# Four different start addresses for the low halves of four groups of weights

## The chip, the core and the metric

The kernel runs on one core of one Trainium2 chip. The metric is the device time of one execution in microseconds (us); the time of a kernel is the median of its runs. Matmuls run on TensorE (PE in the profile, with its weight loads shown apart as PEld), elementwise work on VectorE (DVE) and ScalarE (ACT), and transfers are issued by SyncE (SP).

## The reference, cut to what matters

One decoder layer in float32 for 256 rows of width 2048:

```python
h = rmsnorm(x, pre_mix_gain)
q_sb, k_sb, v_sb, q_dl, k_dl, v_dl = split(h @ w_in)
mixed = concat(head_rmsnorm(stick_breaking(...)), head_rmsnorm(dilated(rope...)))   # 8 + 8 heads of 128
x = x + rmsnorm(mixed @ w_out, post_mix_gain)
h = rmsnorm(x, pre_ffn_gain)
u = causal_depthwise_conv3(h @ w_up) + conv_b        # 2 x 5504 columns: gate and value
f = (gelu(gate) * value) @ w_down
x = x + rmsnorm(f, post_ffn_gain)
```

Only the products `h @ w_in` (its query and key columns) and `h @ w_up` (gate and value) meet the change.

## The kernel before, in words

**Precision by halves.** TensorE multiplies in float32r, a rounded form. To come close to float32, each operand is split into a high part, its value rounded to float32r, and a low part, the rest. A product is then three products: high by high, high by low, low by high. `high` (L86 to L89) makes the high half `wh` of a block of weights on ScalarE, `low` (L91 to L96) the low half `wl` on VectorE, as raw minus high.

**Chunks.** The weights come in chunks of 128 partitions by 2048 columns (two loads of 1024), in the order of the list `chunks` (L169 to L183): value columns of attention (`v`), then query and key for each head (`qk`, where the third entry `s` is 0 for query and 1 for key), then the output projection (`out`), then gate and value for each of 43 blocks of the feed-forward network (`up`, `s` 0 for gate, 1 for value). The main loop (L742) takes them one after another; `ahead` (L187) issues loads two chunks ahead and makes the high and low halves one chunk ahead.

**Which operand is which.** For `v`, `out` and the down projection the weights are the moving operand: they stream through the array in 512 columns, and a 128x128 block of activations is stationary, loaded ahead of each matmul. For `qk` and `up` it is the other way round, in `mm_stationary` (L98 to L107): a 128x128 block of weights is stationary and the transposed activations `hT` move. For each chunk it issues 16 matmuls with blocks of `wh` against 512 moving columns (high and low activations side by side, L103), then 16 with blocks of `wl` against 256 columns (the high activations alone, L107). 32 chunks of `qk` (16 query, 16 key) and 84 of `up` (42 gate, 42 value) go this way; the first gate and value chunk go through `mm_stationary_late` (L109), which mixes blocks of `wh` and `wl` in another order with 256 moving columns each (L113).

**Where the tiles lie.** `hT` holds 2048 bytes for each of 16 row blocks, so every moving operand starts at the same byte modulo 512. Blocks of weights are 512 bytes wide (128 columns of 4 bytes), so the blocks of a tile all start at the same byte modulo 512, too. In the compiled program `hT` starts at byte 384 of the partition, the four `wh` buffers at 57728, 61824, 65920 and 70016, the four `wl` buffers at 74112, 78720, 83328 and 87936: all of them 384 modulo 512. `low` can place its result further into the buffer, by `at` columns; each `wl` buffer has 128 columns (512 bytes) of room for this. Before the change `at` is 80 columns (320 bytes) for `qk` and `up` and 0 for all others. So high blocks lie 0 bytes behind the moving operand and low blocks 320 bytes, modulo 512.

Of the kernel before, what the change touches and what calls it, by code (L numbers as in the profile page):

```python
# [51 lines left out]
def layer_kernel(ctx: ExitStack, tc: tile.TileContext, a, out: bass.AP):  # L52
# [15 lines left out]
            tc.keep_in_program_order(ins)  # L68
        return ins

    HALF, LOW_AT = 1024, 80

    def load(src, w, piece=HALF):
        raws = []
# [7 lines left out]
    def split(raws, kind):  # L82

        return [low(raw, high(raw), kind) for raw in raws]
# [5 lines left out]

    def low(raw, wh, kind=None):  # L91

        at = LOW_AT if kind in ("qk", "up") else 0
        wl = wpool.tile([P, at + raw.shape[1]], F32R, tag="wl", name="wl", bufs=4, padded_shape=[P, HALF + P])[:, at:]
        pin(V.tensor_tensor(wl, raw, wh.bitcast(F32), op=ALU.subtract))  # L95
        return wh, wl  # L96
# [72 lines left out]
    chunks = []  # L169
# [14 lines left out]
    raws, parts_of, between = {}, {}, {}  # L184
    LOADS, SPLITS = 2, 1

    def ahead(i, splits=SPLITS):  # L187
        if i + LOADS >= len(chunks):
            down.load(2 * (i + 1 + LOADS - len(chunks)))
        if i + 1 == len(chunks):  # L190
            down.prepare(2)
        while len(raws) < min(len(chunks), i + 1 + LOADS):
            j = len(raws)
            if j in between:
                nc.sync.dma_start(*between[j])
            raws[j] = load(chunks[j][3], chunks[j][4])
        while len(parts_of) < min(len(chunks), i + 1 + splits):
            j = len(parts_of)
            parts_of[j] = split(raws[j], chunks[j][0])
        return parts_of[i]  # L200


# [82 lines left out]
    for i in range(1, 4):  # L285
        load_x(4 * i, 4 * i + 4)
        for j in range(2 * i, 2 * i + 2):
            raws[j] = load(chunks[j][3], chunks[j][4])
        split_x(4 * i, 4 * i + 4)
        if i == 1:  # L290
            parts_of[2] = split(raws[2], chunks[2][0])
    tc.keep_in_program_order(nc.sync.dma_start(ident, a["cst"][:, C_ID:C_END]))
    between[8] = (x1[:, 0, :], a["x"][0:P, :])
    between[9] = (x1[:, 1, :], a["x"][P:S, :])
# [447 lines left out]
    for i, (kind, p, s, _, w) in enumerate(chunks):  # L742
# [40 lines left out]
        elif kind == "out":  # L783
            if s == 0:
                mm["out", p] = [ps_mm.tile([P, 512], F32, tag="mm", name="mmo") for _ in range(2)]
                if rows is None:
                    nc.sync.dma_start(gbc, a["gpost"][0:1, :].partition_broadcast(P))
                    rows = Rows(mg, "o")
            if p == 3 and s == 2:
                held = parts  # L790
                continue
            if p < 3 or s < 2:
                mm_moving(mm["out", p], parts, mix[0], mix[1], 4 * s, s == 0, s == 3)
                if s == 3:
                    for t in range(2):
                        rows.squares(mm["out", p][t], t, p)
                        rows.take(mm["out", p][t], t, p)
            else:
                pinned[0] = True
                up0 = []  # L800
                r = [None, None]
                sq = Rows(None, "n")

                def square(t, *cs):
                    for c in cs:
                        sq.squares(x1[:, t, col(c)], t, c)

                def keep(t):
                    nc.sync.dma_start(x1_kept[t * P:(t + 1) * P, :], x1[:, t, :])

                pts = {}
                col = lambda c: slice(c * 512, (c + 1) * 512)

                def update(t, c, lo=0, hi=512):
                    cs = slice(c * 512 + lo, c * 512 + hi)
                    pin(V.scalar_tensor_tensor(x1[:, t, cs], mg[:, t, cs], r[t], x1[:, t, cs], op0=ALU.mult, op1=ALU.add))

                def turn(t, b):
                    if b not in pts:
                        pool, tag = (ps_mm, "mm") if b in (4, 5) else (ps_at, "at")  # L820
                        pts[b] = pool.tile([P, 2, S], F32, tag=tag, name="pth")
                    for j in range(2):
                        k = 2 * b + j
                        pin(T.transpose(pts[b][:, j, t * P:(t + 1) * P], x1[:, t, k * P:(k + 1) * P], ident))

                def highs(b):
                    for j in range(2):
                        k = 2 * b + j
                        gp = par[:, P_FFN + k:P_FFN + k + 1]
                        pin(A.activation(hT[0][:, k, :], pts[b][:, j, :], AF.Copy, scale=gp))  # L830

                def lows(b):
                    for j in range(2):
                        k = 2 * b + j
                        gp = par[:, P_FFN + k:P_FFN + k + 1]
                        pin(V.scalar_tensor_tensor(hT[1][:, k, :], pts[b][:, j, :], gp, hT[0][:, k, :].bitcast(F32),
                                                   op0=ALU.mult, op1=ALU.subtract))

                for t in range(2):
                    mm_moving(mm["out", p], held + parts, mix[0], mix[1], 8, False, True, (t,))  # L840
                    if t == 1:
                        for b in range(6):
                            turn(0, b)
                    rows.squares(mm["out", p][t], t, p)
                    vr = rows.mean(t)
                    rows.take(mm["out", p][t], t, p)
                    r[t] = rows.newton(*vr)
                    if t == 0:
                        for c in range(4):
                            update(0, c)  # L850
                        hs = [high(raw) for raw in raws[i + 1]]
                        up0.append(low(raws[i + 1][0], hs[0], "up"))
                        hs.append(high(raws[i + 2][0]))
                        square(0, 0)
                square(0, 1)
                update(1, 0, 0, 256)
                update(1, 0, 256, 512)
                update(1, 1)
                for b in range(2):
                    turn(1, b)  # L860
                    highs(b)
                update(1, 2)
                for b in range(2, 4):
                    turn(1, b)
                    highs(b)
                hs.append(high(raws[i + 2][1]))
                update(1, 3)
                up0.append(low(raws[i + 1][1], hs[1], "up"))
                parts_of[i + 1] = up0
                for b in range(4, 6):  # L870
                    turn(1, b)
                    highs(b)
                    lows(b - 4)
                    for t in range(2):
                        turn(t, b + 2)
                square(0, 2)
                highs(6)
                highs(7)
                square(0, 3)
                raws[i + 3] = load(chunks[i + 3][3], chunks[i + 3][4])  # L880
                hs.append(high(raws[i + 3][0]))
                square(1, 0, 1)
                hs.append(high(raws[i + 3][1]))
                square(1, 2, 3)
                lows(2)
                lows(3)
                parts_of[i + 2] = [low(raws[i + 2][0], hs[2], "up")]
                for b in range(4, 8):
                    lows(b)
                parts_of[i + 2].append(low(raws[i + 2][1], hs[3], "up"))  # L890
                parts_of[i + 3] = [low(raw, h, "up") for raw, h in zip(raws[i + 3], hs[4:])]
                keep(0)
                keep(1)
                pinned[0] = False
                phA.__exit__(None, None, None)
                phB = ctx.enter_context(tc.tile_pool(name="phB", bufs=2))
                yt = [phB.tile([P, len(SINGLES), S], F32R, name=f"yt{i}", bufs=1) for i in range(2)]
                yp = [phB.tile([P, NPAIR, 7, P], F32R, name=f"yp{i}", bufs=1) for i in range(2)]
        else:
            ps = ps_mm.tile([P, 2, S], F32, tag="mm", name="mmu")  # L900
            if p == 0 and s == 0:
                held = [(ps, parts)]
                continue
            if p == 0:
                held.append((ps, parts))
                mm_stationary_late(held, hT2)
                pinned[0] = True
                r2B = second_norm()
                pinned[0] = False
                convolved(held[0][0], 0, 0)  # L910
            else:
                mm_stationary(ps, parts, hT2)
            convolved(ps, p, s)
# [83 lines left out]
```

## Time and profile before

| what | value |
|---|---|
| median of 3 runs | 1103.24 us (1102.65 to 1103.39) |
| profiled execution, its own time | 1103.41 us |
| its span in the profile | 1101.5 us |
| mean granted clock of TensorE | 0.998 |
| PE, PEld, DVE, ACT busy | 99%, 85%, 79%, 61% of the span |
| L103 (high blocks, gate and value) | 1344 matmuls |
| L107 (low blocks, gate and value) | 1344 matmuls |
| L103 and L107, query and key | 512 matmuls each |

Matmuls overlap in the records: a matmul is shown from its start until its last result is out, and the next one starts before that. So the duration of one says little about the pace, and the busy time of a run of n matmuls is n-1 steps from start to start and one duration.

### The profile page before, as it was taken

The numbers are of one execution on the slowest core, as the hardware profiler recorded it, in microseconds if no ns is written. First come the engines' busy times: TensorE is split into PE (matmuls) and PEld (weight loads), VectorE is DVE, ScalarE is ACT, GpSimd is POOL, SyncE is SP. The second block draws the span as 40 slices with busy tenths as digits, with TensorE's granted clock in tenths as the row PEclk, the third lists the DMA queues.
The fourth block names the chain that finished last, engine by engine and source line by source line (L and its number), as shares of the span: only waits on it lengthen the run. The fifth ranks groups of instructions, "written<-read, shape, count | busy, mean of one in ns | idle before, by whom it ended". The sixth has DMA issues, their size and how long they took to land.

```text
span 1101.5 us, 16267 instructions
## 1 busy us (share of the span) xinstructions
PE 1089.8 (99%) x5855; PEld 940.5 (85%) x5855; DVE 872.3 (79%) x1371; ACT 668.0 (61%) x1046; POOL 5.3 (0%) x12
## 2 busy tenths in 40 slices
PE   9999999999999999999999999999999999999996
PEld 6888888888988888888888888888888888888885
DVE  6577776776876588978888878888878898889887
ACT  6656665655654476656666656665556566666665
POOL 0000000000000000000000000000000000000001
PEclk9999999999999999999999999999999999999999
DMA  8978787878889756655555555555556677778775
GB/s 308 385 251 303 254 264 264 289 264 269 290 281 305 260 191 210 191 192 191 192 191 191 191 192 191 189 190 192 184 195 186 192 251 249 249 225 250 246 244 210
DMA packets 75394, 257.80 MB, mean 234 GB/s; under 512 B 8496, under 2 KB 9520, under 8 KB 74544
## 3 DMA queue, kind: packets, MB, share of 16 engines
q1 hardware_dynamic: 74880, 256.22, 69.7%
q8 instruction: 46, 0.75, 0.3%
q10 hardware_dynamic: 432, 0.53, 0.1%
q14 instruction: 36, 0.29, 0.1%
HBM read 238.89 MB, written 17.83 MB: 233 GB/s over the span
## 4 chain that ended last, share of the span: by engine, by line
PE 96%; DMA 1%; ACT 1%; DVE 0%; issue 0%; SPq 0%; DVEq 0%; ACTq 0%
PE mmu L103 28%; PE mmu L107 14%; PE mmqk L103 11%; PE p L626 7%; PE p L625 7%; PE p L624 7%; PE mmqk L107 5%; PE mmo L147 3%; PE mmo L146 3%; PE mmo L150 3%; PE mmv L150 2%; PE mmv L146 2%; PE mmv L147 2%; DMA mg<-in_xT 1%; PE mmu L113 1%; DMA raw<-in_w_v 0%
## 5 line engine op out<-in xcount | busy, mean ns | idle before, releaser
L88 ACT CAST wh<-raw 128x1024 fp32r<-128x1024 f32 (+1 forms) x408 | 413.0, 1024 | 250.9 <-PE mmu L103 118.2
L95 DVE TENSOR_TENSOR wl<-raw,wh 128x1024 fp32r<-128x1024 f32 (+1 forms) x408 | 475.7, 1187 | 90.7 <-ACT wh L88 51.4
L103 PE MATMUL mmu<-hT,wh 128*128 128x512 f32 x1344 | 320.7, 391 | 0.0
L103 PEld LDWEIGHTS mmu<-hT,wh 128*128 128x128 f32 x1344 | 246.9, 188 | 47.7
L107 PEld LDWEIGHTS mmu<-hT,wl 128*128 128x128 f32 x1344 | 170.2, 189 | 6.4
L107 PE MATMUL mmu<-hT,wl 128*128 128x256 f32 x1344 | 172.4, 281 | 0.0
L103 PE MATMUL mmqk<-hT,wh 128*128 128x512 f32 x512 | 125.3, 396 | 0.0
L103 PEld LDWEIGHTS mmqk<-hT,wh 128*128 128x128 f32 x512 | 94.4, 188 | 18.9
L498 DVE SCALAR_TENSOR_TENSOR cv<-u,par,cv 128x255 f32<-128x255 f32 x86 | 41.6, 483 | 68.7 <-ACT cv L497 68.6
L626 PE MATMUL p<-wl,yp 128*128 128x512 f32 x182 | 70.9, 389 | 0.0
L624 PE MATMUL p<-wh,yp 128*128 128x512 f32 x182 | 70.8, 389 | 0.0
L625 PE MATMUL p<-wh,yp 128*128 128x512 f32 x182 | 70.8, 389 | 0.0
L107 PEld LDWEIGHTS mmqk<-hT,wl 128*128 128x128 f32 x512 | 64.8, 189 | 2.4
L107 PE MATMUL mmqk<-hT,wl 128*128 128x256 f32 x512 | 65.5, 281 | 0.0
L497 ACT ACTIVATE cv<-u,par 128x256 f32<-128x256 f32 x86 | 51.3, 597 | 19.7 <-DVE u L495 19.5
L131 ACT COPY half<-mmu 128x256 f32<-128x256 f32 x86 | 32.0, 372 | 41.9 <-PE mmu L107 38.7
L624 PE MATMUL p<-wh,yt 128*128 128x512 f32 (+1 forms) x140 | 53.6, 383 | 0.0
L625 PE MATMUL p<-wh,yt 128*128 128x512 f32 (+1 forms) x140 | 53.6, 383 | 0.0
L626 PE MATMUL p<-wl,yt 128*128 128x512 f32 (+1 forms) x140 | 53.5, 383 | 0.0
L146 PE MATMUL mmv<-wh,hT 128*128 128x512 f32 x128 | 51.1, 400 | 0.4 <-ACT hT L230 0.4
L88 ACT CAST wh<-room 128x1024 fp32r<-128x1024 f32 x26 | 27.4, 1053 | 38.8 <-PE p L625 37.0
L147 PE MATMUL mmv<-wh,hT 128*128 128x512 f32 x128 | 50.2, 392 | 0.3 <-DVE hT L231 0.2
(178 smaller groups left out, 1248.4 us busy)
## 6 DMA issues: line engine op xcount, KB each, us to landing
raw<-in_w_up SPq DMA_DIRECT2D x172, 512.0 KB, 4.3
raw<-in_w_qk SPq DMA_DIRECT2D x64, 512.0 KB, 5.0
raw<-in_w_dn SPq DMA_DIRECT2D x60, 512.0 KB, 4.5
raw<-in_w_o SPq DMA_DIRECT2D x32, 512.0 KB, 5.3
raw<-in_w_v SPq DMA_DIRECT2D x28, 512.0 KB, 5.8
t<-in_w_dn SPq DMA_DIRECT2D x26, 512.0 KB, 5.1
t_kept<-t SPq DMA_DIRECT2D x26, 512.0 KB, 4.0
raw<-t_kept SPq DMA_DIRECT2D x26, 512.0 KB, 4.3
```

Of the source, the lines that this page charges most:

```text
L88: pin(A.copy(wh, raw))
L95: pin(V.tensor_tensor(wl, raw, wh.bitcast(F32), op=ALU.subtract))
L103: T.matmul(ps, wh[:, j * P:(j + 1) * P], h[:, k, :, :], start=(k == 0), stop=False, skip_group_check=True)
L107: T.matmul(ps[:, 0, :], wl[:, j * P:(j + 1) * P], h[:, k, 0, :], start=False, stop=(k == KT - 1), skip_group_check=True)
L146: T.matmul(ps[t], hi[:, k, tc_], ws, start=(first and i == 0 and j == 0), stop=False)
L147: T.matmul(ps[t], lo[:, k, tc_], ws, start=False, stop=False)
L150: T.matmul(ps[t], hi[:, k, tc_], wl[:, j * 512:(j + 1) * 512], start=False, stop=(last and i == len(parts) - 1 and j == n - 1))
L497: A.activation(cv, u, AF.Identity, scale=cw(2), bias=par[:, P_CB + f:P_CB + f + 1])
L498: V.scalar_tensor_tensor(cv[:, 1:], u[:, :S - 1], cw(1), cv[:, 1:], op0=ALU.mult, op1=ALU.add)
L624: T.matmul(ps, yh, wh[:, cs], start=key not in self.begun, stop=False)
L625: T.matmul(ps, yl, wh[:, cs], start=False, stop=False)
L626: T.matmul(ps, yh, wl[:, cs], start=False, stop=self.left[key] == 0)
```

## The change: what it does

The one number `LOW_AT` becomes a table by kind of chunk and `s`: query 32 columns (128 bytes), key 48 (192 bytes), gate 64 (256 bytes), value 112 (448 bytes). `low` looks its argument up there and takes 0 when it is absent, and the callers hand it the pair in place of the kind alone. Buffers, their sizes and count, the order of instructions and the transfers stay as they are.

```diff
-    HALF, LOW_AT = 1024, 80
+    HALF = 1024
+    LOW_AT = {("qk", 0): 32, ("qk", 1): 48, ("up", 0): 64, ("up", 1): 112}
...
     def low(raw, wh, kind=None):
 
-        at = LOW_AT if kind in ("qk", "up") else 0
+        at = LOW_AT.get(kind, 0)
         wl = wpool.tile([P, at + raw.shape[1]], F32R, tag="wl", name="wl", bufs=4, padded_shape=[P, HALF + P])[:, at:]
...
-            parts_of[j] = split(raws[j], chunks[j][0])
+            parts_of[j] = split(raws[j], chunks[j][::2][:2])
...
-                        up0.append(low(raws[i + 1][0], hs[0], "up"))
+                        up0.append(low(raws[i + 1][0], hs[0], ("up", 0)))
...
-                parts_of[i + 2].append(low(raws[i + 2][1], hs[3], "up"))
-                parts_of[i + 3] = [low(raw, h, "up") for raw, h in zip(raws[i + 3], hs[4:])]
+                parts_of[i + 2].append(low(raws[i + 2][1], hs[3], ("up", 1)))
+                parts_of[i + 3] = [low(raw, h, ("up", 0)) for raw, h in zip(raws[i + 3], hs[4:])]
```

The remaining lines of the diff are the same replacement at the other calls.

More of the change, by code (lines that the diff above doesn't have):

```diff
@@ L290, in layer_kernel @@
         if i == 1:
-            parts_of[2] = split(raws[2], chunks[2][0])
+            parts_of[2] = split(raws[2], chunks[2][::2][:2])
     tc.keep_in_program_order(nc.sync.dma_start(ident, a["cst"][:, C_ID:C_END]))
@@ L867, in layer_kernel @@
                 update(1, 3)
-                up0.append(low(raws[i + 1][1], hs[1], "up"))
+                up0.append(low(raws[i + 1][1], hs[1], ("up", 0)))
                 parts_of[i + 1] = up0
@@ L886, in layer_kernel @@
                 lows(3)
-                parts_of[i + 2] = [low(raws[i + 2][0], hs[2], "up")]
+                parts_of[i + 2] = [low(raws[i + 2][0], hs[2], ("up", 1))]
                 for b in range(4, 8):
                     lows(b)
-                parts_of[i + 2].append(low(raws[i + 2][1], hs[3], "up"))
-                parts_of[i + 3] = [low(raw, h, "up") for raw, h in zip(raws[i + 3], hs[4:])]
+                parts_of[i + 2].append(low(raws[i + 2][1], hs[3], ("up", 1)))
+                parts_of[i + 3] = [low(raw, h, ("up", 0)) for raw, h in zip(raws[i + 3], hs[4:])]
                 keep(0)
```

## The prediction

> **What bounds the kernel now.** I read the page first, then the waits of TensorE, then the stretch in which gate and value are computed, then single runs of matmuls in the timeline.
>
> ```profile
> span 1101.5 us, 16267 instructions
> ...
> PE 1089.8 (99%) x5855; PEld 940.5 (85%) x5855; DVE 872.3 (79%) x1371; ACT 668.0 (61%) x1046; POOL 5.3 (0%) x12
> ...
> PE 96%; DMA 1%; ACT 1%; DVE 0%; issue 0%; SPq 0%; DVEq 0%; ACTq 0%
> PE mmu L103 28%; PE mmu L107 14%; PE mmqk L103 11%; PE p L626 7%; PE p L625 7%; PE p L624 7%; PE mmqk L107 5%; PE mmo L147 3%; PE mmo L146 3%; PE mmo L150 3%; PE mmv L150 2%; PE mmv L146 2%; PE mmv L147 2%; DMA mg<-in_xT 1%; PE mmu L113 1%; DMA raw<-in_w_v 0%
> ```
>
> ```profile
> PE idle L239 <- DVE warm L236: 1.2, 1, 1.2
> PE pth L824 <- DVE x L816: 1.2, 1, 1.2
> PE mmv L146 <- ACT hT L230: 0.4, 1, 0.4
> PE mmv L147 <- DVE hT L231: 0.2, 1, 0.2
> PE mmu L113 <- ACT hT L830: 0.2, 1, 0.2
> ```
>
> The chain that ended last is 96% TensorE, and the low blocks of L107, the only instructions whose operands the change moves, hold 14% and 5% of it. TensorE's idle waits in the list come to 3.2 us in all. So a change of the matmul pace reaches the end one to one as long as the others keep up. In the gate and value stage they do:
>
> ```profile
> 416.00:876.00 460.00, 460.00 (x2660) 406.42 (x2659) 379.22 (x633) 278.55 (x408) 0.00 (x0) 1.00 0.58 190
> ```
>
> Of 460 us VectorE (the third busy column) works 379.22 (82%), ScalarE 278.55, the DMA engines 58%, at a granted clock of 1.00. A gain of a few per cent stays covered by this slack.
>
> **The pace, and what the address has to do with it.** Each matmul has a weight load of its own, issued while the matmul before it streams. Two readers thus go through the same memory side by side: the moving operand and the next block of weights. The busy time of a run of n matmuls is n-1 steps and one duration. For the gate and value stage the groups give the duration, the timeline the runs:
>
> ```profile
> L103 PE MATMUL mmu<-hT,wh 128*128 128x512 f32 x1344 | 320.7, 391 | 0.0
> L107 PE MATMUL mmu<-hT,wl 128*128 128x256 f32 x1344 | 172.4, 281 | 0.0
> L107 PE MATMUL mmqk<-hT,wl 128*128 128x256 f32 x512 | 65.5, 281 | 0.0
> ```
>
> ```profile
> 520.06 2.05 PE L107 MATMUL mmu<-hT,wl 128*128 128x256 f32 x16
> 521.95 3.81 PE L103 MATMUL mmu<-hT,wh 128*128 128x512 f32 x16
> 525.60 2.05 PE L107 MATMUL mmu<-hT,wl 128*128 128x256 f32 x16
> ```
>
> Low blocks, 320 bytes behind: (2.05 - 0.281) / 15 = 117.9 ns a step; the 32 runs of query and key give (65.5 / 32 - 0.281) / 15 = 117.7. High blocks, 0 bytes behind, 512 columns: (3.81 - 0.391) / 15 = 227.9.
>
> The first gate and value chunk (L113) is the one place where blocks at 0 and at 320 bytes meet the same moving operand of 256 columns; the attention stage has one odd run:
>
> ```profile
> 404.68 1.07 PE L113 MATMUL mmu<-hT,wl 128*128 128x256 f32 x8
> 405.59 4.00 PE L113 MATMUL mmu<-hT,wh 128*128 128x256 f32 x32
> 409.43 1.11 PE L113 MATMUL mmu<-hT,wl 128*128 128x256 f32 x8
> ```
>
> ```profile
> 60.42 1.98 PE L107 MATMUL mmqk<-hT,wl 128*128 128x256 f32 x16
> 62.24 3.81 PE L103 MATMUL mmqk<-hT,wh 128*128 128x512 f32 x16
> 65.89 2.05 PE L107 MATMUL mmqk<-hT,wl 128*128 128x256 f32 x16
> ```
>
> At 0 bytes 32 matmuls take 4.00 us: (4.00 - 0.283) / 31 = 119.9 ns, with 0.283 us as one duration (the low ones' 0.281 would give the same to 0.1 ns). At 320 bytes there are two paces: 117.9 in nearly all runs, and 113 in two, the one at 60.42 ((1.98 - 0.28) / 15 = 113.3) and the one at 404.68 ((1.07 - 0.28) / 7 = 112.9). A run keeps its pace from end to end. So the distance of the two readers matters, by some 2 ns between 0 and 320 bytes, and at one and the same distance the way in which a run is entered decides between two paces 4.6 ns apart.
>
> How far down could it go? At distance 0, 256 more columns cost 227.9 - 119.9 = 108.0 ns; that is what 256 columns take without a load of their own. So the surcharge of a weight load is 11.9 ns at 0 bytes, 9.9 or 5.3 at 320, and none at all would be 108.0.
>
> The Trainium skill's page "TensorE: Matmul & The Clock Gate", section "Part 2: What happens when you issue a matmul", holds that TensorE has two independent read ports, so that loading the next weights takes nothing from the running matmul; by that rule alone the distance would be worth nothing and the time would stay at 1103.2 us. The rows 113, 117.9 and 119.9 for the same shape speak against it.
>
> **The change part by part.**
>
> *The subtract that writes the low half.* It writes to another start in the same buffer. In the gate and value stage it starts 320 bytes in, in the down projection (from `room`) at 0:
>
> ```profile
> L95 DVE TENSOR_TENSOR wl<-raw,wh 128x1024 fp32r<-128x1024 f32 x167 | 199.6, 1219 | 5.4 <-PE mmu L107 5.4
> ```
>
> ```profile
> L95 DVE TENSOR_TENSOR wl<-room,wh 128x1024 fp32r<-128x1024 f32 x26 | 31.8, 1224 | 14.2 <-ACT wh L88 14.0
> ```
>
> 1219 and 1224 ns: the start is worth nothing there, and VectorE's slack would cover 5 ns anyway. No instruction, transfer, wait or buffer is added, moved or removed; the queues are as before.
>
> *The low matmuls.* A step counts where the next load is a low block too: 15 of 16 in a run (the 16th loads a high block, still at 0). Query and key have 16 runs each, 240 steps; gate and value 42 each, 630 steps; in all 1740, besides some 30 in L113 that I leave out. One ns on each is 1.74 us of the end. The bounds from rows: all at 119.9, 2.0 x 1740 = +3.5 us; all at 113.3, -4.6 x 1740 = -8.0; no surcharge at all, -9.9 x 1740 = -17.2. Upwards no row sets an end; I take one step more of the size that lies between 113.3 and 119.9, that is 126.5 or +8.6 ns, +15.0 us were it all four groups.
>
> *Which value at which distance.* No row shows 128, 192, 256 or 448 bytes. I take each from the nearest rows on the circle of 512 bytes, in proportion: from 0 (119.9) to 320 (117.9), 128 lies at 119.1, 192 at 118.7, 256 at 118.3; from 320 on to 512, which is 0 again, 448 lies at 119.2. Against 117.9 that is 1.2 x 240 + 0.8 x 240 + 0.4 x 630 + 1.3 x 630 = 0.29 + 0.19 + 0.25 + 0.82 = +1.6 us. I choose the usual pace of 117.9 for 320 bytes and not 113, since it stands in all but two of the runs.
>
> *The high run behind a low one.* The run at 62.24, behind the odd fast one, takes 3.81 us as the run at 521.95 behind a usual one: no price is carried over, and I set it to nothing. Its own steps, 228 ns, are above the 226.7 of the rows
>
> ```profile
> 899.97 0.39 PE L625 MATMUL p<-wh,yt 128*128 128x512 f32 x1
> ...
> 901.33 0.39 PE L625 MATMUL p<-wh,yt 128*128 128x512 f32 x1
> ```
>
> (1.36 us for 6 steps), so entering such a run costs some 1.2 x 15 = 18 ns; if a new phase doubled or removed this on 116 runs, it would be 2.1 us either way, an end that the range keeps.
>
> The sum: the profiled execution took 1103.41 us, its span 1101.5 and 1.9 around it, 0.17 above the median of 1103.24. The span becomes 1103.1, the profiled time 1105.0, and the median 1103.24 + 1.6 = 1104.8.
>
> **The rivals.** About 0.2% (2.2 us) is what a measurement of this kernel can tell from no change; that is 1.3 ns on the mean step.
>
> *Forecast, 0.40: all four distances cost between 117.9 and 119.9.* Its own range is 1103.2 to 1106.8. With the values of the sum it stays below 2.2 us; with gate and value near 119.9 it passes. I give 0.27 to same, 0.13 to slower.
>
> *Distance is worth nothing at these values, 0.10, same.* The moving operand reads 1024 bytes while the load reads 512; it gains 512 bytes on it whatever the start and so meets it once. Then only equal starts (two half meetings) are special, and 117.9 holds: 1103.2. Against it: the same distance already shows two paces.
>
> *Gate or value falls into the fast pace, 0.27, nearly all faster.* 113.3 exists at 320 bytes, and what decides is where the two readers stand at the entry of a run; another distance may lead every run there. One of the two groups: -4.6 x 630 = -2.9 us, 1100.3. Both: 1097.4. All four: 1095.2. If one of them falls and the other rises to 119.9 (+1.3), it is same: 0.02. For it speaks that all of L107 repeats the same step run after run, so a whole group would change at once. Against it: two runs of 118 only.
>
> *The readers stay in each other's way longer, 0.23, slower.* At 448 bytes the block starts 64 bytes short of a full circle, so just behind the moving operand, at 128 just ahead of it, where the faster reader runs into the load early and may be held back for more of it. If gate or value took 126.5 ns, it is +8.6 x 630 = +5.4 us, 1108.6; both, 1114.1. It decides from +1.3 ns on the mean of all steps, or +3.5 ns on one of the two large groups. Nothing in the rows goes above 119.9 for undisturbed runs of this shape, which is why it has less than the forecast. 0.22 to slower, 0.01 to same.
>
> That the change doesn't do what it says can be left out: the new starts are constants in the slice, and every call of `low` for these groups hands over the pair.
>
> **How the numbers follow.** Faster 0.25; same 0.27 + 0.10 + 0.02 + 0.01 = 0.40; slower 0.13 + 0.22 = 0.35. The predicted time is the forecast's, 1104.8. The range reaches down to 1098.0, which takes in one large group in the fast pace and 2.1 us of cheaper entries, and up to 1109.5, one large group at 126.5 and a little of the rest; outside are both large groups fast or both slow, and no surcharge at all (1086.0).
>
> **What would show it right or wrong.** In the changed kernel's timeline the runs of 16 of L107 give the pace of each group by themselves: busy (2.05 us now) less 0.281, over 15. Right: query 2.07, key 2.06, gate 2.06, value 2.07, all between 2.05 and 2.08, with L103 at 3.81 and L95 at 1.22 us as before. A run of 1.98 is the fast pace, one of 2.18 the slow one. Wrong altogether would be L103 steps that change, waits of TensorE beyond the 3.2 us, or the four groups at one pace while the time moves.

## The result and the profile after

The changed kernel takes 1106.24 us (1105.86 to 1106.62), the kernel before 1103.01 us on the same occasions: a ratio of 1.003 with a 95% interval of 1.002 to 1.0039. It is slower by 3.2 us, and the interval leaves no change out.

The page of the changed kernel, span, engines and chain (every line of the code after the table has moved down by one, so L103 is L104, L107 is L108, L95 is L96):

```profile
span 1104.0 us, 16267 instructions
...
PE 1092.0 (99%) x5855; PEld 941.8 (85%) x5855; DVE 871.9 (79%) x1371; ACT 668.0 (61%) x1046; POOL 5.3 (0%) x12
...
PE 98%; DMA 0%; DVE 0%; ACT 0%; issue 0%; SPq 0%; DVEq 0%; ACTq 0%
```

The same instructions, and TensorE still holds the chain: the 2.5 us of span were added inside TensorE's work. The groups of the changed kernel show where (count, busy us, mean ns of one):

```profile
L104 PE MATMUL mmu<-hT,wh 128*128 128x512 f32 x1344 | 322.3, 392 | 0.0
L108 PE MATMUL mmu<-hT,wl 128*128 128x256 f32 x1344 | 173.4, 281 | 0.0
L104 PE MATMUL mmqk<-hT,wh 128*128 128x512 f32 x512 | 125.3, 396 | 0.0
L108 PE MATMUL mmqk<-hT,wl 128*128 128x256 f32 x512 | 66.1, 281 | 0.0
```

Against the rows of before, the low matmuls grew by 1.0 us (172.4 to 173.4) in gate and value and by 0.6 (65.5 to 66.1) in query and key. But the high matmuls of gate and value, which the change does not touch, grew by 1.6 (320.7 to 322.3). Together that is 3.2 us, as much as the medians differ. The spans of the two profiled executions differ by 2.5 us only: this one reached its first query matmul 0.4 us earlier (50.37 us against 50.80), ahead of all that the change touches, and 0.3 us of overlap and rounding of the groups was not worked out. The high matmuls of query and key stayed where they were before:

```profile
L103 PE MATMUL mmqk<-hT,wh 128*128 128x512 f32 x512 | 125.3, 396 | 0.0
```

Which group pays is read from single runs in the timeline of the changed kernel, where each run of 16 stands with its start and its busy time. First a query and the key behind it, with the high run between them left out, then a value, a gate and a value:

```profile
104.93 2.08 PE L108 MATMUL mmqk<-hT,wl 128*128 128x256 f32 x16
...
111.99 2.05 PE L108 MATMUL mmqk<-hT,wl 128*128 128x256 f32 x16
```

```profile
600.51 3.85 PE L104 MATMUL mmu<-hT,wh 128*128 128x512 f32 x16
604.20 2.08 PE L108 MATMUL mmu<-hT,wl 128*128 128x256 f32 x16
606.11 3.81 PE L104 MATMUL mmu<-hT,wh 128*128 128x512 f32 x16
609.77 2.05 PE L108 MATMUL mmu<-hT,wl 128*128 128x256 f32 x16
```

Query at 128 bytes takes 2.08 (120 ns a step), key at 192 the old 2.05. Gate at 256 takes 2.08, and value at 448 the old 2.05; but the high run behind a value run (the one at 600.51) takes 3.85 where it took 3.81. By the starts in the trace it needs ten steps (241, 238, 233, 236, 224 and so on) until it settles at 227 ns, where a high run of before needs five (233, 236, 228, 233, 230). In attention only 6 of the 32 high runs start right behind a low run, the others behind matmuls of another kind, and so their group shows nothing of this. One value run, the first whole one, went at the fast pace, and the high run behind it took 3.82:

```profile
420.49 1.98 PE L108 MATMUL mmu<-hT,wl 128*128 128x256 f32 x16
422.31 3.82 PE L104 MATMUL mmu<-hT,wh 128*128 128x512 f32 x16
```

The subtract that writes the low half is as it was:

```profile
L96 DVE TENSOR_TENSOR wl<-raw,wh 128x1024 fp32r<-128x1024 f32 x166 | 198.2, 1218 | 5.3 <-PE mmu L108 5.3
```

### The profile page after: what moved, and what is told of

Same layout as the page of the kernel before. It is cut to its first block, busy times and chain, and to the rows that moved or that the text cites. A ratio compares the mean times of both kernels' runs of the same rounds, so it can differ in the third digit from the quotient of the medians.

```text
span 1104.0 us, 16267 instructions
## 1 busy us (share of the span) xinstructions
PE 1092.0 (99%) x5855; PEld 941.8 (85%) x5855; DVE 871.9 (79%) x1371; ACT 668.0 (61%) x1046; POOL 5.3 (0%) x12
## 4 chain that ended last, share of the span: by engine, by line
PE 98%; DMA 0%; DVE 0%; ACT 0%; issue 0%; SPq 0%; DVEq 0%; ACTq 0%
PE mmu L104 28%; PE mmu L108 14%; PE mmqk L104 11%; PE p L626 7%; PE p L625 7%; PE p L627 7%; PE mmqk L108 6%; PE mmo L147 3%; PE mmo L151 3%; PE mmo L148 3%; PE mmv L148 3%; PE mmv L151 3%; PE mmv L147 3%; PE mmu L114 1%; DMA raw<-in_w_v 0%; PE po L344 0%
## 5 line engine op out<-in xcount | busy, mean ns | idle before, releaser
L96 DVE TENSOR_TENSOR wl<-raw,wh 128x1024 fp32r<-128x1024 f32 (+1 forms) x408 | 475.3, 1186 | 91.7 <-ACT wh L89 51.9
L104 PE MATMUL mmu<-hT,wh 128*128 128x512 f32 x1344 | 322.3, 392 | 0.0
L104 PEld LDWEIGHTS mmu<-hT,wh 128*128 128x128 f32 x1344 | 246.7, 188 | 49.3
L108 PEld LDWEIGHTS mmu<-hT,wl 128*128 128x128 f32 x1344 | 171.2, 189 | 6.5
L108 PE MATMUL mmu<-hT,wl 128*128 128x256 f32 x1344 | 173.4, 281 | 0.0
L104 PE MATMUL mmqk<-hT,wh 128*128 128x512 f32 x512 | 125.3, 396 | 0.0
L104 PEld LDWEIGHTS mmqk<-hT,wh 128*128 128x128 f32 x512 | 94.3, 188 | 18.8
L108 PEld LDWEIGHTS mmqk<-hT,wl 128*128 128x128 f32 x512 | 65.4, 188 | 2.5
L108 PE MATMUL mmqk<-hT,wl 128*128 128x256 f32 x512 | 66.1, 281 | 0.0
```

The lines of the kernel that those rows point to most:

```text
L104: T.matmul(ps, wh[:, j * P:(j + 1) * P], h[:, k, :, :], start=(k == 0), stop=False, skip_group_check=True)
L108: T.matmul(ps[:, 0, :], wl[:, j * P:(j + 1) * P], h[:, k, 0, :], start=False, stop=(k == KT - 1), skip_group_check=True)
```

## The experiments

The theory to test: the distance of the low block behind the moving operand sets both the pace of the low steps and the way in which the next high run is entered. The first rival: it is the group, or its place in the order of chunks; the second: it is the address by itself. All kernels below are the changed kernel with the edit shown.

**One distance for all four groups.** Four kernels, each with one number in the table:

```diff
-    LOW_AT = {("qk", 0): 32, ("qk", 1): 48, ("up", 0): 64, ("up", 1): 112}
+    LOW_AT = {("qk", 0): 32, ("qk", 1): 32, ("up", 0): 32, ("up", 1): 32}     # all_128; 48, 64 and 112 for the others
```

The four expectations give the paces to the wrong distances: one high run of the attention stage is cut in two by matmuls of another kind, and counting it twice had exchanged query with key and gate with value. So they attach the paces of 192 to 128 and those of 448 to 256, and the reverse.

> All four groups at 128 bytes. Theory (the distance alone sets the pace and the entry of the next high run, as the query runs of the changed kernel show it): low steps 117.8 ns in every group, high runs 3.65 us, so the time of before, 1103.0 us. Rival (the group or its place in the chunk order sets it, key and value being slow for another reason): key steps 120.5, value 119.5 again and 1106.2 us.

> All four groups at 192 bytes. Theory: 120.5 ns a low step everywhere, +2.7 ns on 1740 steps, +4.7 us: 1107.7 us. Rival (the group decides): 1106.2 us, query and gate at 117.8.

> All four groups at 256 bytes. Theory: 117.8 ns a low step everywhere, and the high run behind each low run 37 ns longer (3.69 us for 16 steps in place of 3.65): 116 x 0.037 = +4.3 us less 0.3 for the shorter last step, 1107.0 us. Rival (the longer high run belongs to the value chunk, whatever the distance): only the 42 value chunks pay, +1.5 us, 1104.5 us.

> All four groups at 448 bytes. Theory: a first step of 114 and then 120, 119.5 on the mean of 15, +1.7 ns on 1740 steps, +3.0 us, and high runs of 3.65 us: 1106.0 us. Rival (the group decides): 1106.2 us but with query at 117.8 and key at 120.5; the times can't tell, the paces can.

Measured: all_128 1106.76 us (ratio 1.0032, 1.002 to 1.0044), all_192 1105.86 (1.0025, 1.0015 to 1.0035), all_256 1105.93 (1.0027, 1.0017 to 1.0038), all_448 1105.87 (1.0026, 1.0016 to 1.0036), all beside 1103.15 of before. As numbers the first three were missed, by 3.8, 1.8 and 1.1 us, and for all_128 and all_192 the rival's 1106.2 came nearer than the theory's time; what decides between them is the pace of each group. The groups of all_128, all_192, all_256 and all_448, in this order:

```profile
L104 PE MATMUL mmu<-hT,wh 128*128 128x512 f32 x1344 | 320.0, 390 | 0.0
L108 PE MATMUL mmu<-hT,wl 128*128 128x256 f32 x1344 | 175.4, 283 | 0.0
...
L108 PE MATMUL mmqk<-hT,wl 128*128 128x256 f32 x512 | 66.7, 283 | 0.0
```

```profile
L104 PE MATMUL mmu<-hT,wh 128*128 128x512 f32 x1344 | 323.7, 393 | 0.0
L108 PE MATMUL mmu<-hT,wl 128*128 128x256 f32 x1344 | 172.2, 279 | 0.0
...
L108 PE MATMUL mmqk<-hT,wl 128*128 128x256 f32 x512 | 65.5, 279 | 0.0
```

```profile
L104 PE MATMUL mmu<-hT,wh 128*128 128x512 f32 x1344 | 320.8, 391 | 0.0
L108 PE MATMUL mmu<-hT,wl 128*128 128x256 f32 x1344 | 174.6, 283 | 0.0
...
L108 PE MATMUL mmqk<-hT,wl 128*128 128x256 f32 x512 | 66.4, 283 | 0.0
```

```profile
L104 PE MATMUL mmu<-hT,wh 128*128 128x512 f32 x1344 | 323.7, 393 | 0.0
L108 PE MATMUL mmu<-hT,wl 128*128 128x256 f32 x1344 | 172.2, 279 | 0.0
...
L108 PE MATMUL mmqk<-hT,wl 128*128 128x256 f32 x512 | 65.5, 279 | 0.0
```

From the mmqk rows a step is (66.7 / 32 - 0.283) / 15 = 120.1 ns at 128, 117.9 at 192, 119.5 at 256 and 117.9 at 448, and the mmu rows agree within 0.3 ns. By the starts in the traces the means are 120.5, 117.8, 119.5 and 117.8, in query, key, gate and value alike. So the distance decides and the group does not; the first rival is out. There are two kinds of price. 128 and 256 cost low steps: 175.4 against 172.4 of before, 3.0 us, and 1.2 in attention, less 0.7 in the high runs, makes 3.5 of the 3.6 us of all_128. 192 and 448 keep the low pace, and pay the whole of it in the high runs of gate and value: 323.7 against 320.7, 3.0 us. Their rows are the same to the last digit.

**More distances, and the modulus.** Since each group shows its own pace, one kernel tests four distances:

```diff
-    LOW_AT = {("qk", 0): 32, ("qk", 1): 48, ("up", 0): 64, ("up", 1): 112}
+    LOW_AT = {("qk", 0): 16, ("qk", 1): 96, ("up", 0): 8, ("up", 1): 24}      # scan_a
+    LOW_AT = {("qk", 0): 104, ("qk", 1): 120, ("up", 0): 0, ("up", 1): 4}     # scan_c
```

> Query at 64 bytes, key at 384, gate at 32, value at 96. The runs so far, by the order of the chunks: 128 bytes 120.5 ns a low step, 192 and 448 both 117.8 (with a high run behind of 3.69 us in place of 3.65), 256 119.5, 320 117.8, 0 119.9. Theory (the pattern repeats every 256 bytes): 64 goes as 320, 117.8; 384 as 128, 120.5 with the steps 124, 120, 123, 117. Rival (every distance within 512 has its own pace): the two lie more than 1 ns from that. 32 and 96 are new: if only whole 64-byte blocks count, 32 goes as 0 (119.5 to 120) and 96 as 64.

> Query at 416 bytes, key at 480, gate at 0, value at 16. Theory (256 bytes repeat): gate at 0 goes as 256 did in its runs, a first step of 114, then 120, 119.5 on the mean. Rival (512): 0 differs from that by more than 1 ns. If only whole 64-byte blocks count, 16 goes as 0, 416 as 384 (120.5), 480 as 448 (117.8); if finer ones count, 16 lies between or elsewhere.

Measured: single runs of 1104.61 and 1105.52 beside 1102.88 of before. The timelines, scan_a with query (64), key (384), then gate (32) and value (96); scan_c with query (416), key (480), then gate (0) and value (16):

```profile
104.84 2.05 PE L108 MATMUL mmqk<-hT,wl 128*128 128x256 f32 x16
...
111.89 2.09 PE L108 MATMUL mmqk<-hT,wl 128*128 128x256 f32 x16
```

```profile
603.80 2.05 PE L108 MATMUL mmu<-hT,wl 128*128 128x256 f32 x16
...
609.37 2.04 PE L108 MATMUL mmu<-hT,wl 128*128 128x256 f32 x16
```

```profile
104.88 2.08 PE L108 MATMUL mmqk<-hT,wl 128*128 128x256 f32 x16
...
111.96 2.03 PE L108 MATMUL mmqk<-hT,wl 128*128 128x256 f32 x16
```

```profile
604.08 2.08 PE L108 MATMUL mmu<-hT,wl 128*128 128x256 f32 x16
...
609.64 2.06 PE L108 MATMUL mmu<-hT,wl 128*128 128x256 f32 x16
```

64 goes as 320 (2.05), 384 as 128 (2.08 to 2.09), 0 as 256 (2.08): with 192 and 448 that is four pairs, 256 bytes apart, each with one pace. The busy times alone do not tell 128 from 256, but the steps one by one do, and they agree within each pair: 124, 120, 123, 117 and so on at 128 and at 384, a first step of 114 and then 120 at 256 and at 0. The rival of 512 bytes is out. The theory that only whole blocks of 64 bytes count is out too: by the starts 32 and 16 take 118.3 and 118.2 ns and do not go as 0 (119.5), and 416 takes 119.7 where 384 takes 120.5. The best of the new ones, 480, is 0.02 us a run below the usual 2.05, on 16 key runs too little to show in the time.

**Distance or address.** In all_later the activations and all weight buffers lie 128 bytes further on, with their distances kept; in moving_later only the moving operand and, by the table, the low blocks (a last part of that edit, not shown, takes the 128 bytes back for `room`, a later use of the same buffer).

```diff
+    G.memset(cpool.tile([P, 32], F32, name="gap"), 0.0)                       # all_later
     hT2 = cpool.tile([P, KT, 2, S], F32R, tag="hT", name="hT")
...
-    gpre = small.tile([P, KT], F32, name="gpre", bufs=1, padded_shape=[P, KT + 32])
+    gpre = small.tile([P, KT], F32, name="gpre", bufs=1, padded_shape=[P, KT])
```

```diff
-    LOW_AT = {("qk", 0): 32, ("qk", 1): 48, ("up", 0): 64, ("up", 1): 112}
+    LOW_AT = {("qk", 0): 64, ("qk", 1): 80, ("up", 0): 96, ("up", 1): 16}     # moving_later
...
-    hT2 = cpool.tile([P, KT, 2, S], F32R, tag="hT", name="hT")
+    hT2 = cpool.tile([P, 32 + KT * 2 * S], F32R, tag="hT", name="hT")[:, 32:].rearrange("p (k i s) -> p k i s", k=KT, i=2)
...
-    rstd1 = cpool.tile([P, 2], F32, name="rstd1", padded_shape=[P, 2 + 112])
+    rstd1 = cpool.tile([P, 2], F32, name="rstd1", padded_shape=[P, 2 + 112 - 32])
```

> The activations and all weight buffers lie 128 bytes further on, every distance between them as in the changed kernel. Theory (only distances count): paces 120.5, 117.8, 119.5, 117.8, high runs behind value 3.69 us. Rival (the address by itself counts): the low blocks now lie where 256, 320, 384 and 64 bytes put them, so query 119.5, and gate and value other than 119.5 and 117.8. The output and down projections meet their activations at another distance here, so their matmuls, and the time, may move for that.

> The moving operand is put 128 bytes further on, and the low blocks 128 bytes with it (their distances of the changed kernel are kept: 128, 192, 256, 448); the high blocks stay and so lie 384 bytes behind it. Theory (the distance to the moving operand sets the pace): query 120.5, key 117.8, gate 119.5, value 117.8 a low step, as in the changed kernel. Rival (the address of the low blocks by itself, or against the high blocks and the raw weights): what that address gave before, that is 256 bytes for query 119.5, 320 for key 117.8, 384 for gate, 64 for value. The high runs may change, since their distance does.

Measured: single runs, all_later 1112.88 us, moving_later 1113.91, beside 1102.88. The groups of all_later, then those of moving_later:

```profile
L104 PE MATMUL mmu<-hT,wh 128*128 128x512 f32 x1344 | 322.3, 392 | 0.0
L108 PE MATMUL mmu<-hT,wl 128*128 128x256 f32 x1344 | 173.3, 281 | 0.0
...
L626 PE MATMUL p<-wh,yp 128*128 128x512 f32 x182 | 71.8, 395 | 0.0
```

```profile
L104 PE MATMUL mmu<-hT,wh 128*128 128x512 f32 x1344 | 326.8, 395 | 0.0
L108 PE MATMUL mmu<-hT,wl 128*128 128x256 f32 x1344 | 173.3, 281 | 0.0
```

In all_later both operands of these matmuls lie 128 bytes further on, and the two mmu rows are those of the changed kernel (322.3; 173.4); the steps one by one are the same, too. So for this shift only the distance counts, and the second rival is out. The 10 us that all_later loses lie elsewhere: the output and down projections now read activations 384 bytes behind their moving weights. Such a matmul is shown with 395 ns; before it was 389:

```profile
L624 PE MATMUL p<-wh,yp 128*128 128x512 f32 x182 | 70.8, 389 | 0.0
```

By the starts in the traces the step of the down projection grows from 226.8 to 232.4 ns, and that of the output as much: 5.6 ns on each of the 384 of the output and the 942 of the down projection are 7.4 us, and with the 3.2 of the change itself 10.6 against the 10.0 measured. moving_later settles less. Its high blocks, whose address did not move, got slower when the operand that moves past them was shifted: 326.8 against 322.3. But the low paces come out mixed: by the starts in the trace 118.6 ns for query, neither the theory's 120.5 nor the rival's 119.5, and 118.9 for gate, neither 119.5 nor the 120.5 that 384 bytes gave. Its high runs no longer settle at one step, so the low runs are entered in other ways; that this is the reason was not tested.

**The way in which a run is entered.** The two paces at 320 bytes were still unexplained. all_448 had a case of the fast one, in the first feed-forward chunk, behind steps of 256 columns (timeline of all_448):

```profile
405.12 3.99 PE L114 MATMUL mmu<-hT,wh 128*128 128x256 f32 x32
408.95 1.07 PE L114 MATMUL mmu<-hT,wl 128*128 128x256 f32 x8
409.86 3.81 PE L104 MATMUL mmu<-hT,wh 128*128 128x512 f32 x16
```

(1.07 - 0.28) / 7 = 113, and the high run behind it takes 3.81, where 448 bytes otherwise cost 3.85. In the kernel before, the same place at 320 bytes gave 1.11. If the entry decides, the end of each high run can be shaped for it: the last one or two high blocks are multiplied in two halves of 256 columns, the same products with one more weight load each.

```diff
-                T.matmul(ps, wh[:, j * P:(j + 1) * P], h[:, k, :, :], start=(k == 0), stop=False, skip_group_check=True)
+                for part in ((0, 1) if k >= KT - 2 else (slice(0, 2),)):
+                    T.matmul(ps[:, part, :], wh[:, j * P:(j + 1) * P], h[:, k, part, :], start=(k == 0), stop=False, skip_group_check=True)
```

Here with two blocks in halves; halves_1_at_448 has `KT - 1`, and the table holds one distance for all: 112 columns, 80 for halves_2_at_320, 48 for halves_2_at_192.

> All four groups at 448 bytes, and the last high block of each run multiplied in two halves of 256 columns (the same products, one more weight load), so that a low run is entered from steps of 256 columns. Theory (the entry decides between the two paces; at 448, entered from such steps in the first feed-forward chunk, eight low steps in a row took 113 to 114 ns): low steps 113.3, -4.5 x 15 = -67 ns a chunk, high runs back at 3.65 us, +5 to +13 ns for the halves: some -55 ns x 116 = -6.4 us against 1103.1, 1096.7 us. Rival (the fast pace comes only after a wait or a long run of equal steps): 117.8 as in all_448 and 5 to 13 ns more a chunk, 1106.5 to 1107.4 us.

> As halves_1_at_448 with the last two high blocks in halves, in case one pair of halves doesn't settle. Theory: 113.3 a low step, +18 ns a chunk for the halves: (-67 + 18) x 116 = -5.7 us, 1097.4 us. Rival: 117.8 and 1108.0 us.

> The same halves with the distance of before, 320 bytes. In the first feed-forward chunk the low run at 320 was entered from steps of 256 columns too and went at 117.8. Theory (distance and entry together decide): 117.8, +18 ns x 116 = +2.1 us, 1105.2 us. Rival (the entry alone decides): 113.3, 1097.4 us.

> As halves_2_at_448 with all four groups at 192 bytes, 256 less. Theory (the pattern repeats every 256 bytes, so only the distance modulo 256 counts, in the fast pace too): 113.3 a low step and the time of halves_2_at_448, 1097.6 us. Rival (448 is special within 512, since it lies 64 bytes short of the next start): 117.8 as at 320, 1105 us.

Measured, beside 1103.09 of before for the first three: halves_1_at_448 1102.27 us (ratio 0.9993, 0.9984 to 1.0001), halves_2_at_448 1097.60 (0.9948, 0.9934 to 0.9962), halves_2_at_320 1104.85 (1.0016, 1.0008 to 1.0025); halves_2_at_192 1097.73 beside 1103.03 (0.9949, 0.9935 to 0.9962). Their timelines in the same order:

```profile
602.80 2.04 PE L109 MATMUL mmu<-hT,wl 128*128 128x256 f32 x16
604.68 3.81 PE L105 MATMUL mmu<-hT,wh 128*128 128x512 f32 x17
```

```profile
600.00 1.98 PE L109 MATMUL mmu<-hT,wl 128*128 128x256 f32 x16
601.81 3.83 PE L105 MATMUL mmu<-hT,wh 128*128 128x512 f32 x18
605.48 1.98 PE L109 MATMUL mmu<-hT,wl 128*128 128x256 f32 x16
```

```profile
606.25 3.83 PE L105 MATMUL mmu<-hT,wh 128*128 128x512 f32 x18
609.92 2.05 PE L109 MATMUL mmu<-hT,wl 128*128 128x256 f32 x16
```

```profile
599.99 1.98 PE L109 MATMUL mmu<-hT,wl 128*128 128x256 f32 x16
601.81 3.84 PE L105 MATMUL mmu<-hT,wh 128*128 128x512 f32 x18
605.48 1.98 PE L109 MATMUL mmu<-hT,wl 128*128 128x256 f32 x16
```

Two pairs of halves and 448 or 192 bytes: every low run shown takes 1.98 us, (1.98 - 0.28) / 15 = 113.3 ns a step, and so do all but two (at 448) or one (at 192) of the 115 runs that the traces show in one piece. By the groups of halves_2_at_448 the low matmuls lose 8.0 us against before (172.4 to 166.5 in gate and value, 65.5 to 63.4 in query and key) and the high ones, with 232 more, gain 2.2 (320.7 to 322.4, 125.3 to 125.8): 5.8 us less, against 5.5 in the time. All three kernels with two pairs came within 0.4 us of their theories' times. The same entry at 320 bytes keeps 2.05 (but for two runs in the whole trace), and one pair alone at 448 keeps 2.04: neither the entry nor the distance does it alone. So halves_1_at_448 missed its 1096.7 us; it is still 3.6 us below all_448, since the high run behind, though one matmul longer, takes 3.81 us and not 3.85. That says something of the theory, too: distance and low pace (117.8) are those of all_448, and yet the high runs settle after two steps (233, 231) and not after ten. So the price of a high run isn't set by the distance alone either; what differs ahead of it is how the low run was entered. Two pairs at 448 or 192 beat the kernel before by half a per cent.

## Why the prediction was right where it was, and wrong where it was

The direction held, and the time lies within the range and within the forecast's own range of 1103.2 to 1106.8. But +1.6 us was forecast and +3.2 came, twice as much. The likeliest outcome was no measurable change, which the prediction put at up to 2.2 us, and the time came out just beyond it, as the forecast had it for gate and value near 119.9; gate alone went there. That all of it would lie in TensorE's pace, with the subtract at 1.22 us and nothing else moved, held (1218 ns).

Two of its steps failed and were partly made good by chance. By its own signs it was wrong in part: query and gate went to 2.08 and key and value stayed at 2.05, all within the 2.05 to 2.08 that it named, but it had called L103 steps that change "wrong altogether", and those behind the value runs did.

*Which value at which distance.* Taking each from the nearest rows on a circle of 512 bytes was wrong. The pattern repeats after 256 bytes, and between 0 (119.5) and 128 (120.1 to 120.5) lies 64 at 117.9: it is no slope. In place of +0.29, +0.19, +0.25 and +0.82 us for query, key, gate and value, the low runs gave about +0.6 (the mmqk row, query alone, since key kept 2.05), 0, +1.0 (the mmu row, gate alone) and 0. The total of these, 1.6, is that of the forecast only because its errors cancel.

*The high run behind a low one.* "No price is carried over, and I set it to nothing" was the term that failed. The row it rested on was one run behind a fast run at 320 bytes. Behind 448 bytes the high run costs some 40 ns more (3.85 against 3.81; 36 by the starts), some 40 times, which is nearly all of the +1.6 us of the high rows: half of the whole loss. The end that the prediction kept for this, 18 ns on 116 runs or 2.1 us, was near by luck: the price is twice as high, and only the gate and value runs and 6 of attention start right behind a low run.

The floor of 108.0 ns, on which only an end outside the range hung, was a little high: it took the mean high step of 227.9, slower first steps included; with the settled 226.7 it is 106.8.

The rival of the longer collision, priced at 126.5 ns, did not come: 448 has the old pace, and 128, the slowest of the four, 120.5. The rival of the fast pace came in one value run (the 1.98 at 420.49) and in no group, but the experiments show that its reason was right: the entry decides, together with the distance. The rival that distance is worth nothing fell, and with it, for these matmuls, the Trainium skill's rule in "TensorE: Matmul & The Clock Gate" ("Part 2: What happens when you issue a matmul") that the next weight load takes nothing from the running matmul: for one shape the steps were 113.3, 117.9, 119.5 and 120.1 ns with nothing changed but addresses and the entry.

What stays open is the mechanism below this: why 256 bytes, and why a run that has found a step keeps it. The runs show when it happens; what in the memory or the array does it was not measured.

## What to carry to other kernels

Where TensorE is the bound and every matmul has its own weight load, the distance of the stationary block behind the moving operand, modulo 256 bytes here, is worth measuring: in this kernel it is a few ns on each of some thousand matmuls, and one kernel with several distances shows several paces in one trace. Judge a setting by the run that it touches and by the run behind it, since half of the price can fall there. When one and the same setting shows two paces, look at how the runs are entered before taking either as its price.

## What the runs showed of the hardware that was not expected

- For matmuls of 512 columns the distance counts as well: with the stationary block 384 bytes behind, the down projection's matmuls take 395 ns in place of 389 at 0 (all_later; 232.4 in place of 226.8 from start to start), and the high runs 3.88 to 3.90 us in place of 3.81 (moving_later, here its timeline).

```profile
600.30 3.88 PE L104 MATMUL mmu<-hT,wh 128*128 128x512 f32 x16
...
605.90 3.90 PE L104 MATMUL mmu<-hT,wh 128*128 128x512 f32 x16
```

- More instructions can be faster: halves_2_at_448 issues 232 matmuls more than the kernel before (two in each of 116 chunks) and is 5.5 us shorter, since they put the low runs into the step of 113.3 ns.
